# A rotation kernel: the last 2 MB loaded by two transfers, and slabs 2 and 3 stored in 1 MB halves

## Chip, cores, metric

One core of a Trainium2 chip. The metric is the device time of one execution in microseconds (us); below, "time" is the median of the runs of one kernel. A transfer is carried by 16 DMA engines in packets, and has landed when all 16 have reported; SyncE is the engine that issues the transfers, HBM the memory that holds the arrays, PSUM a second on-chip memory. The profile's own span is about 1.8 us shorter than the device time.

## The reference

```python
x = np.random.randn(32, 3, 256, 256).astype(np.float32)      # 25.17 MB
out = np.rot90(x, k=-1, axes=(-2, -1))                       # each 256 x 256 image turned by 90 degrees
```

Nothing is computed. Each byte is read once and written once: 50.33 MB in all, plus the rearranging between.

## The kernel before

The 96 images are handled as twelve slabs of 2 MB. Each slab has its own on-chip buffer, so all loads can be issued at once. VectorE transposes slab n into the buffer of slab n-1, whose contents it has already used; slab 0 goes to PSUM and is copied back at the very end, over the buffer of the last slab.

```python
    for n in range(n_slabs):                      # loads
        if n == last:
            nc.sync.dma_start(out=units[n], in_=ld8_v[n])            # 2 MB, two 8 KB rows per partition
            continue
        for i in range(I):                                           # I = 2: 1 MB each
            if n == 0:
                nc.sync.dma_start(out=units[n][:, i], in_=ld8_v[n][:, i])          # 128 x 8 KB
            else:
                nc.sync.dma_start(out=units[n][i::I]..., in_=ld16_v[n, i])         # 64 x 16 KB

    for n in range(n_slabs):
        ...                                       # two VectorE transposes: t_in -> t_out
        if n == 1:                                # stores
            nc.sync.dma_start(out=st_v[n][:, 0, :W], in_=t_out[:, 0, :W])          # 128 KB
            nc.sync.dma_start(out=st_v[n][:, 0, W:], in_=t_out[:, 0, W:])          # 896 KB
            nc.sync.dma_start(out=st_v[n][:, 1], in_=t_out[:, 1])                  # 1 MB
        elif n:
            nc.sync.dma_start(out=st_v[n], in_=t_out)                              # 2 MB

    for i in range(I):
        nc.scalar.copy(out=units[last][:, i], in_=turned0[:, i])
    nc.sync.dma_start(out=st_v[0], in_=units[last])
```

(Three dots mark cuts.) All transfers are issued by SyncE in this order. The built program gives them eight completion semaphores in turn, so each issue first waits until the transfer eight places earlier has landed.

Of the kernel before, what the change touches and what calls it, by code (L numbers as in the profile page):

```python
# [1 line left out]

# [4 lines left out]




@with_exitstack
def kernel(
    ctx: ExitStack,
    tc: tile.TileContext,
    x: bass.AP,
    out: bass.AP,
):

















    nc = tc.nc
    fp32 = mybir.dt.float32

    B, C, H, W = x.shape
    P = nc.NUM_PARTITIONS  # L40
    RI, RO = 16, 8
    K = H // RI
    I = 2
    Q = P // (K * I)
    n_slabs = B * C // (Q * I)
    last = n_slabs - 1
    F = RO * W

    rows_in = x.rearrange("b c h w -> (b c h) w")
    rows_out = out.rearrange("b c h w -> (b c h) w")  # L50
    ld8_v = rows_in.rearrange("(n i p r) w -> n p i (r w)", i=I, p=P, r=RO)
    ld16_v = rows_in.rearrange("(n i m r) w -> n i m (r w)", i=I, m=Q * K, r=RI)
    st_v = rows_out.rearrange("(n i p c) w -> n p i (c w)", i=I, p=P, c=RO)

    pools = [ctx.enter_context(tc.tile_pool(name=f"unit{u}", bufs=1)) for u in range(n_slabs)]
    units = [pool.tile([P, I, F], fp32, name=f"u{u}") for u, pool in enumerate(pools)]
    psum = ctx.enter_context(tc.tile_pool(name="psum", bufs=1, space=bass.MemoryType.PSUM))
    turned0 = psum.tile([P, I, F], fp32, name="turned0")

    for n in range(n_slabs):  # L60
        if n == last:
            nc.sync.dma_start(out=units[n], in_=ld8_v[n])
            continue
        for i in range(I):
            if n == 0:
                nc.sync.dma_start(out=units[n][:, i], in_=ld8_v[n][:, i])  # L66
            else:
                nc.sync.dma_start(out=units[n][i::I].rearrange("p i f -> p (i f)"), in_=ld16_v[n, i])

    for n in range(n_slabs):  # L70
        t_in, t_out = units[n], units[n - 1] if n else turned0
        if n in (0, last):
            for i in range(I):
                src = t_in[:, i].rearrange("p (r g c) -> p c r g", r=RO, c=RO)
                dst = t_out[:, i].rearrange("p (c g r) -> p c r g", c=RO, r=RO)
                nc.vector.transpose(out=dst[:, :, ::-1, ::-1], in_=src)  # L76
        else:
            src = t_in.rearrange("p i f -> p (i f)").rearrange("p (r g c) -> p c r g", r=RI, c=RO)
            dst = t_out.rearrange("p i (c k r) -> p c r k i", c=RO, r=RI)[:, :, ::-1, ::-1, :]
            for h in range(2):  # L80
                cs = slice(h * RO // 2, (h + 1) * RO // 2)
                nc.vector.transpose(out=dst[:, cs], in_=src[:, cs])  # L82

        if n == 1:
            nc.sync.dma_start(out=st_v[n][:, 0, :W], in_=t_out[:, 0, :W])
            nc.sync.dma_start(out=st_v[n][:, 0, W:], in_=t_out[:, 0, W:])
            nc.sync.dma_start(out=st_v[n][:, 1], in_=t_out[:, 1])
        elif n:
            nc.sync.dma_start(out=st_v[n], in_=t_out)  # L89

# [5 lines that stand above are left out]
# [1 line left out]
_INS = ['x']  # L97
_OUTS = [((32, 3, 256, 256), 'float32')]


# [23 lines left out]
```

## Time and profile before

| | before |
|---|---|
| time, us | 124.06 (3 runs, 123.96 to 124.23) |
| DMA engines busy | 97.8% |
| VectorE busy | 76% |
| transfers | 37 (23 loads, 14 stores) |
| last store issued, landed, us | 101.15, 121.18 |

Read the DMA share and the GB/s per slice first: they show whether the bytes flow without a break. Then read who issues the transfers and what each issue waits for. The lines for that are in the prediction. One view it names without showing it is the chain of waits, of the kernel before, by engine:

```profile
DMA 57%; DVE 13%; issue 7%; DVEq 3%; ACT 2%; SPq 1%
```

### The profile page before, as it was taken

The numbers are of one execution on the slowest core, as the hardware profiler recorded it, in microseconds if no ns is written. First come the engines' busy times: TensorE is split into PE (matmuls) and PEld (weight loads), VectorE is DVE, ScalarE is ACT, GpSimd is POOL, SyncE is SP. The second block draws the span as 40 slices with busy tenths as digits, with TensorE's granted clock in tenths as the row PEclk, the third lists the DMA queues.
The fourth block names the chain that finished last, engine by engine and source line by source line (L and its number), as shares of the span: only waits on it lengthen the run. The fifth ranks groups of instructions, "written<-read, shape, count | busy, mean of one in ns | idle before, by whom it ended". The sixth has DMA issues, their size and how long they took to land.

```text
span 122.2 us, 134 instructions
## 1 busy us (share of the span) xinstructions
DVE 93.3 (76%) x24; ACT 5.0 (4%) x3; POOL 0.2 (0%) x4
## 2 busy tenths in 40 slices
DVE  0299999999999999999999999999999940000000
ACT  0000000000000000000040000000000651000000
POOL 0000000000000000000000000000000000000000
DMA  3999999999999999999999999999999999999993
GB/s 88 429 432 434 440 440 429 429 429 429 429 429 429 429 429 424 434 424 408 370 414 428 426 429 429 429 429 429 429 429 429 424 429 429 429 429 426 429 429 166
DMA packets 5584, 50.33 MB, mean 412 GB/s; under 512 B 592, under 2 KB 720, under 8 KB 848
## 3 DMA queue, kind: packets, MB, share of 16 engines
q1 hardware_dynamic: 5584, 50.33, 97.8%
HBM read 25.17 MB, written 25.17 MB: 412 GB/s over the span
## 4 chain that ended last, share of the span: by engine, by line
DMA 57%; DVE 13%; issue 7%; DVEq 3%; ACT 2%; SPq 1%
DMA u<-in_x_dram 39%; DMA out_dram<-u 18%; DVE u L82 10%; DVE u L76 3%; DVEq L119 3%; ACT u L92 2%; SPq L66 1%; SPq L89 0%
## 5 line engine op out<-in xcount | busy, mean ns | idle before, releaser
L82 DVE STREAM_TRANSPOSE u<-u 128x2048 f32<-128x2048 f32 x20 | 78.0, 3948 | 0.3
L76 DVE STREAM_TRANSPOSE turned<-u 128x2048 f32<-128x2048 f32 x2 | 7.6, 3828 | 5.5 <-DMA u<-in_x_dram 5.5
L76 DVE STREAM_TRANSPOSE u<-u 128x2048 f32<-128x2048 f32 x2 | 7.8, 3953 | 0.0
L92 ACT COPY u<-turned 128x2048 f32<-128x2048 f32 x2 | 3.7, 1866 | 33.8 <-DVE u L76 33.8
L92 ACT ACT_TABLE_LOAD x1 | 1.3, 1283 | 62.4 <-DMA u<-in_x_dram 62.4
L108 POOL MEMSET const-bfloat16-1.0<- 128x1 bf16 x1 | 0.1, 102 | 0.0
L108 POOL MEMSET const-uint8-127<- 128x1 uint8 x1 | 0.1, 102 | 0.0
L108 POOL MEMSET const-float32-0.0<- 128x1 f32 x1 | 0.1, 99 | 0.2 <-issue 0.2
L108 POOL MEMSET const-float32-1.0<- 128x1 f32 x1 | 0.1, 99 | 0.0
## 6 DMA issues: line engine op xcount, KB each, us to landing
u<-in_x_dram SPq DMA_DIRECT2D x22, 1024.0 KB, 19.6
out_dram<-u SPq DMA_DIRECT2D x11, 2048.0 KB, 25.0
u<-in_x_dram SPq DMA_DIRECT2D x1, 2048.0 KB, 22.5
out_dram<-u SPq DMA_DIRECT2D x1, 1024.0 KB, 20.2
out_dram<-u SPq DMA_DIRECT2D x1, 896.0 KB, 20.2
out_dram<-u SPq DMA_DIRECT2D x1, 128.0 KB, 20.6
```

Of the source, the lines that this page charges most:

```text
L66: nc.sync.dma_start(out=units[n][:, i], in_=ld8_v[n][:, i])
L76: nc.vector.transpose(out=dst[:, :, ::-1, ::-1], in_=src)
L82: nc.vector.transpose(out=dst[:, cs], in_=src[:, cs])
L92: nc.scalar.copy(out=units[last][:, i], in_=turned0[:, i])
L108: nc = _bacc.Bacc("TRN2", target_bir_lowering=False, num_devices=1)
L119: with _tile.TileContext(nc) as tc:
```

## The change

In the kernel before, the 2 MB load is one entry in the rotation of eight, and so are the 2 MB stores behind it. The change cuts that load and the stores of slabs 2 and 3 into 1 MB halves, so that SyncE meets transfers of one size while the work turns from loading to storing, and half of the last slab is announced earlier.

```diff
@@ -58,11 +58,8 @@
     turned0 = psum.tile([P, I, F], fp32, name="turned0")
 
     for n in range(n_slabs):
-        if n == last:
-            nc.sync.dma_start(out=units[n], in_=ld8_v[n])
-            continue
         for i in range(I):
-            if n == 0:
+            if n in (0, last):
                 nc.sync.dma_start(out=units[n][:, i], in_=ld8_v[n][:, i])
             else:
                 nc.sync.dma_start(out=units[n][i::I].rearrange("p i f -> p (i f)"), in_=ld16_v[n, i])
@@ -85,6 +82,9 @@
             nc.sync.dma_start(out=st_v[n][:, 0, :W], in_=t_out[:, 0, :W])
             nc.sync.dma_start(out=st_v[n][:, 0, W:], in_=t_out[:, 0, W:])
             nc.sync.dma_start(out=st_v[n][:, 1], in_=t_out[:, 1])
+        elif n in (2, 3):
+            for i in range(I):
+                nc.sync.dma_start(out=st_v[n][:, i], in_=t_out[:, i])
         elif n:
             nc.sync.dma_start(out=st_v[n], in_=t_out)
```

## The prediction

> **What bounds the kernel now.** I began with the busy summary, the slices and the queue totals of the page, because a kernel that only rearranges data is either bound by its transfers or by the engine that rearranges.
>
> ```profile
> DVE 93.3 (76%) x24; ACT 5.0 (4%) x3; POOL 0.2 (0%) x4
> DMA  3999999999999999999999999999999999999993
> GB/s 88 429 432 434 440 440 429 429 429 429 429 429 429 429 429 424 434 424 408 370 414 428 426 429 429 429 429 429 429 429 429 424 429 429 429 429 426 429 429 166
> DMA packets 5584, 50.33 MB, mean 412 GB/s; under 512 B 592, under 2 KB 720, under 8 KB 848
> q1 hardware_dynamic: 5584, 50.33, 97.8%
> ```
>
> The 16 DMA engines are busy for 97.8% of the span and hold 429 GB/s in nearly every slice; VectorE is busy for 76%. 50.33 MB at 429 GB/s take 117.3 us of the 122.2 us span. The other 4.9 us are all that better scheduling of the same bytes could get, and the slices say where they lie. The first slice (3.05 us) moves at 88 instead of 429 GB/s and so loses 2.4 us; the last one, at 166, loses 1.9 us. In the middle there is one dip, slices 18 to 22 counted from one (424, 408, 370, 414, 428): 101 GB/s short in total, 101/429 of a slice, 0.7 us. Part of that is bookkeeping, since a packet is counted where it starts; finer windows give the real size:
>
> ```profile
> 20.00:54.00 34.00, 33.83 (x10) 0.00 (x0) 0.00 (x0) 1.00 1.01 432
> 59.00:61.50 2.50, 2.46 (x2) 0.00 (x0) 0.00 (x0) 1.00 0.96 342
> 64.00:101.00 37.00, 35.09 (x10) 3.61 (x2) 0.00 (x0) 1.00 1.01 428
> ```
>
> (Stretch, its length, VectorE, ScalarE, GpSimd, clock, DMA share, GB/s.) Loads alone run at 432, stores alone at 428, and the 2.5 us at the end of the last load run at 342: 2.5 x (1 - 342/428) = 0.50 us lost. The DMA share stays at 0.96 there, so the engines are not without work; their packets take longer. The packet records agree: an 8 KB packet takes 309 ns nearly everywhere, and 359 and 416 ns on average of those that start between 59 and 60 and between 60 and 61 us. The completion times say it too: 1 MB loads land 2.45 us apart, the last of them at 56.89, and the 2 MB load at 62.29, 5.40 us later instead of 4.90.
>
> Next I read the issue order, which is where the change acts. All transfers go through SyncE, in program order, on eight completion semaphores used in turn, so that transfer k is issued only when transfer k-8 has landed. Single windows of the timeline:
>
> ```profile
> 49.60 0.38 SPq L89 DMA_DIRECT2D out_dram<-u  x1
> 52.06 0.38 SPq L89 DMA_DIRECT2D out_dram<-u  x1
> 54.51 2.09 SPq L89 DMA_DIRECT2D out_dram<-u  x1
> 56.95 2.13 SPq L89 DMA_DIRECT2D out_dram<-u  x1
> 62.35 1.51 SPq L89 DMA_DIRECT2D out_dram<-u  x1
> 75.80 0.37 SPq L89 DMA_DIRECT2D out_dram<-u  x1
> 101.15 0.37 SPq L93 DMA_DIRECT2D out_dram<-u  x1
> ```
>
> The issue of a store takes 0.37 to 0.38 us, but those of slabs 4, 5 and 6 take 2.09, 2.13 and 1.51 us. These are the three issues with most still queued: counting packets issued and not yet finished, 1392 were in flight after the quick issue at 52.06, and 1510, 1654 and 1545 after the slow ones, whose end comes as earlier packets drain. I read this as a queue that is full at some 1400 to 1600 packets. It holds up SyncE; whether it also has to do with the slow packets at 59 to 61 us, the profile does not say.
>
> Last, the waits of SyncE and the end. The final store is issued at 101.15, after VectorE's last slab (99.2) and ScalarE's copy, and lands at 121.18: it stands 20 us in the queue behind stores issued earlier.
>
> ```profile
> SPq L119 <- DMA out_dram<-u: 19.7, 1, 19.7
> SPq L89 <- DVE u L82: 26.3, 5, 7.4
> ```
>
> So VectorE, ScalarE and SyncE all finish 20 us ahead, and the end is simply when the queue has carried its bytes. The chain of waits on the page, which puts 13% on VectorE and 7% on "issue", follows releases back and does not contradict this: that time lies under queued transfers.
>
> **What the Trainium skill says.** "DMA: Bandwidth & Descriptors", section Where 436 GB/s comes from, gives 435 GB/s as the ceiling of the 16 engines' ports. The trace agrees: 428 to 432 in steady state, 98 to 99% of it. Its section Rules for kernel authors asks for 128 partitions and at least 1 MiB per transfer; the new pieces are exactly 1 MB over 128 partitions, and the trace has such transfers already (both loads of slab 0, and the store of the second half of slab 1: landing 2.46 and 2.43 us after the one before, that is at full rate). "Perfetto Trace Analysis", section DMA Optimizations, says that splitting may help where DMA engines are generally idle; here they are not. The section Queues, rings and completion order of the first page describes completion as one semaphore write per engine, after that engine's data. The trace shows 592 packets under 512 B = 37 transfers x 16, each of 4 B and 9 ns.
>
> **The change part by part.** The order of instructions on VectorE is unchanged. SyncE issues 40 transfers instead of 37: the last load as 2 x 1 MB, slabs 2 and 3 as 2 x 1 MB each (the first stored slab was in pieces already). Bytes, 8 KB packets and addresses are the same; only the order of the two halves of a row pair within an engine's share may differ.
>
> Added on the queue: 3 transfers x 1 completion packet per engine x 9 ns = 0.03 us. This is on the path, and is all the direct cost.
>
> Added on SyncE: 3 issues x some 0.37 us = 1.1 us, beside the queue and with 20 us of slack at the end: 0.
>
> Moved: the stores. Three more entries in the rotation make every later store wait for a more recent transfer. Landings at 2.45 us per MB (slot 22 at 56.9; the halves of the last load at about 59.4 and 61.9) give: the first three stores at about 44.7, 47.1 and 49.6 (before 42.3, 44.7, 47.1), the halves of slabs 2 and 3 at 52.0, 54.5, 56.9 and 59.4, slab 4 at about 61.9 (before 54.5), slab 5 at about 62.6 (before 56.9), slab 6 at about 64.6 (before 62.35), slab 7 at 68.0, when VectorE has it. From there VectorE's 7.85 us per slab (2 x 3.9) sets the issue as before: 75.8, 83.6, 91.5, 99.2, and 101.15 for slab 0. Does the queue run dry? When the loads end, slabs 1 to 3 are issued: 6 MB, 14.7 us of work, up to about 76.5. By 68.0 slabs 4 to 7 are in, which reach to about 96; slab 8 is in at 75.8, and so on. It never comes within 10 us of empty. So the delay of slabs 4 to 6 costs nothing.
>
> Removed: the crowding. At about 59.4 us I count 24 to 31 outstanding, 8 x 144 = some 1150 packets less those done, and with slabs 4 and 5 issued about 1300 to 1400. The two long issues at 54.5 and 56.9 should go; a shorter one may come at about 64.6 for slab 6, where seven outstanding and the new one come to near 1500.
>
> Sum: +0.03 us, and between 0 and -0.5 us for the dip, according to whether the slow packets come from the crowded queue (or from the 2 MB load's order) or from the turn from loads to stores, which stays. I give the removal about one chance in three: 0.03 - 0.33 x 0.5 = -0.14 us, so 124.06 becomes about 123.9.
>
> **The rivals.**
> First, the dip goes entirely. For it: the slow packets begin at 59.3 us, just after the two slowest issues, and they belong to the one load that has two rows per partition. Against it: the first ten packets of each engine of that load run at 311 to 314 ns while the queue is as full, and the stores with the same two-row shape take 309 ns. It would make 123.5 to 123.6 us.
>
> Second, nothing changes in the queue: the slow packets are the last three to five loads of each engine, just where the engine's next work is stores, and the turn has to be made in either kernel. That makes 124.1 us. It is my main case.
>
> Third, a new wait: the rotation of eight now spans less data, so SyncE reaches each store later. A starved queue would need the 14.7 us of stores at hand at 62 us to run out before slab 4 comes at 62, which the waits make impossible; only a store issued over 10 us late would show, and VectorE is ahead until 68 us. I see no way to 2% (2.5 us) here. A smaller loss, 0.2 to 0.4 us, could come if VectorE's and the transfers' traffic met differently at the turn.
>
> Fourth, the earlier arrival of half of the last slab helps VectorE. It cannot: VectorE turns to that slab at 91.5 us, and the load has landed at 62.3.
>
> **Range and chances.** A gain of over 2% would have to bring the time below 121.6 us; even with the dip gone the queue carries 117.3 us of bytes and the ramps at both ends stay. A loss of over 2% needs 2.5 us without work for the DMA engines. Three runs of before spread over 0.27 us. So 123.9 us, 123.4 (dip gone and a favourable run) to 124.4 (no gain and a small loss at the turn); within 2% nearly certainly.
>
> **What would show it.** Steps right: 640 packets under 512 B instead of 592; a queue share of about 98%; the last store issued at about 101.2 and landing some 20 us later; issues of slabs 4 and 5 at about 62 us; slices of 429 GB/s outside the middle. The long issues of SyncE gone or later. The slices around 59 to 61 us decide between the first two rivals: near 429 there means the crowding (or the order in the load) made the dip, near 370 means the turn. The prediction is wrong if a slice after the middle falls well below 429 (starvation), or if 8 KB packets of the split transfers take other than 309 ns.

## The result, and the profile after

| | before | after |
|---|---|---|
| time, us (6 runs each, in the same rounds) | 124.09 (123.96 to 124.23) | 123.97 (123.77 to 124.08) |
| ratio after / before | | 0.9988, 95% interval 0.9975 to 1.0001 |
| transfers | 37 | 40 |
| packets under 512 B | 592 | 640 |
| last store issued, landed, us | 101.15, 121.18 | 101.27, 121.46 |

A ratio is the mean time of one kernel's fast runs over that of the other's of the same rounds, so it is not quite the ratio of the medians quoted beside it. The page of the changed kernel:

```profile
DVE 93.3 (76%) x24; ACT 5.0 (4%) x3; POOL 0.2 (0%) x4
DMA  3999999999999999999999999999999999999994
GB/s 118 418 450 429 429 429 429 429 429 429 429 429 429 429 429 429 429 429 391 359 413 429 429 429 426 429 421 429 429 429 429 429 429 429 429 429 426 429 429 180
DMA packets 5632, 50.33 MB, mean 412 GB/s; under 512 B 640, under 2 KB 768, under 8 KB 896
q1 hardware_dynamic: 5632, 50.33, 97.8%
DVE 47%; issue 27%; DMA 4%; DVEq 3%; ACT 2%
```

The dip is where it was (391, 359, 413), and the rest is at 429 as before. The last line is the chain of waits again: it now puts 47% on VectorE and 4% on transfers, although nothing about the end has changed. The chain follows whatever released the last issue, and the issues of SyncE are released now by a landing, now by VectorE; here it happened to stay on VectorE all the way back. A chain that runs underneath a full queue is not a bound.

The three stretches that the prediction read, now of the kernel after (stretch, length, VectorE, ScalarE, GpSimd, clock, DMA share, GB/s):

```profile
20.00:54.00 34.00, 33.83 (x10) 0.00 (x0) 0.00 (x0) 1.00 1.00 424
59.00:61.50 2.50, 2.47 (x2) 1.28 (x1) 0.00 (x0) 1.00 1.01 330
64.00:101.00 37.00, 35.21 (x10) 3.48 (x2) 0.00 (x0) 1.00 1.01 428
```

330 against 342 GB/s: the slow stretch at the end of the loads is still there. The completion times agree: the second half of the last load lands 2.99 us after the first half, where other 1 MB loads take 2.45. So 0.54 us is lost there, against 0.50 before. (The 424 in the first row is a matter of where packets start: up to 49.8 us the loads still land 2.44 to 2.54 us apart.)

The issue of the stores of slabs 4, 5, 6, 7, 8 and 0, from single windows of the timeline of the kernel after:

```profile
62.67 0.39 SPq L89 DMA_DIRECT2D out_dram<-u  x1
63.27 0.54 SPq L89 DMA_DIRECT2D out_dram<-u  x1
65.21 0.77 SPq L89 DMA_DIRECT2D out_dram<-u  x1
68.08 2.31 SPq L89 DMA_DIRECT2D out_dram<-u  x1
75.91 0.37 SPq L89 DMA_DIRECT2D out_dram<-u  x1
101.27 0.37 SPq L93 DMA_DIRECT2D out_dram<-u  x1
```

Slab 4 is issued 8.2 us later than before (62.67 instead of 54.51) and slab 5 6.3 us later, at no cost, since the queue is full of earlier stores. The two issues of over 2 us at 54.5 and 56.95 are gone. One of 2.31 us has appeared at 68.08, again at no cost.

### The profile page after: what moved, and what is told of

Same layout as the page of the kernel before. It is cut to its first block, busy times and chain, and to the rows that moved or that the text cites. A ratio compares the mean times of both kernels' runs of the same rounds, so it can differ in the third digit from the quotient of the medians.

```text
span 122.3 us, 138 instructions
## 1 busy us (share of the span) xinstructions
DVE 93.3 (76%) x24; ACT 5.0 (4%) x3; POOL 0.2 (0%) x4
## 3 DMA queue, kind: packets, MB, share of 16 engines
q1 hardware_dynamic: 5632, 50.33, 97.8%
## 4 chain that ended last, share of the span: by engine, by line
DVE 47%; issue 27%; DMA 4%; DVEq 3%; ACT 2%
DVE u L79 37%; DVE turned L73 6%; DMA u<-in_x_dram 4%; DVE u L73 3%; DVEq L119 3%; ACT u L92 2%
```

## The experiments

Twelve runs followed: ten new kernels, and the kernel after and one of the new ones once more; all gave the right result. A number used throughout is the **excess of the last load**: how much later it lands than the load before it, less 2.45 us for 1 MB or 4.90 us for 2 MB. A load has landed when the slowest of the 16 engines has finished its share, so the excess follows the slowest engine. "In flight" counts the packets issued and not yet finished.

### 1. Only the load split (load_only)

```diff
# against the kernel after
-        elif n in (2, 3):
-            for i in range(I):
-                nc.sync.dma_start(out=st_v[n][:, i], in_=t_out[:, i])
```

> Only the last load is split; all stores of slabs 2 to 11 stay at 2 MB. Turn theory (the slow load packets come from the change from loads to stores and cost 0.5 us in any kernel): the last 1 MB load lands 2.9 to 3.0 us after the one before it, time 124.0 to 124.1. Row-order theory (alternating between the two halves of the 2 MB load slows its packets): the last two loads land 2.45 us apart each, time 123.5 to 123.6. Crowding theory: the queue is still crowded, so the dip stays too; long issues of SyncE of over 1.5 us remain.

123.89 us against 123.87 for before in the same rounds, ratio 0.9999 (0.9981 to 1.0017). The last load lands 2.81 us after the one before: excess 0.36 us. So it is not the alternation between two rows of a partition that slows the packets. One expectation missed: only one long issue was left, of 1.17 us at 62.43. The issue of slab 5 at 59.61 took 0.37 us although 1621 packets were in flight after it. In the kernel before, an issue that ended at 1510 took 2.09 us. So "the queue is full at 1400 to 1600 packets" is not the rule behind the long issues.

### 2. Only the stores split (store_only)

```diff
# against the kernel before
+        elif n in (2, 3):
+            for i in range(I):
+                nc.sync.dma_start(out=st_v[n][:, i], in_=t_out[:, i])
         elif n:
```

> Only slabs 2 and 3 are stored in halves; the last load stays one 2 MB transfer. Turn theory: the 2 MB load lands about 5.4 us after the load before, time 124.0 to 124.1. Crowding theory: as the queue holds less by then, the dip shrinks below 0.3 us, time below 123.9.

123.80 us, ratio 0.9991 (0.9974 to 1.0008). The 2 MB load lands 5.30 us after the load before, excess 0.40 us, although at most 1237 packets were in flight until it had landed, instead of 1654. The slow packets stay without the crowd. The time is where the crowding theory had it (below 123.9 us), but so is that of the kernel before in these rounds (123.87 us), so it decides nothing.

### 3. Every store in halves (all_halves)

```diff
# against the kernel after; slab 0's store is split likewise
-        elif n in (2, 3):
+        elif n > 1:
             for i in range(I):
                 nc.sync.dma_start(out=st_v[n][:, i], in_=t_out[:, i])
-        elif n:
-            nc.sync.dma_start(out=st_v[n], in_=t_out)
```

> The change taken further: every store in 1 MB halves, 48 transfers with the last load split. At most 8 x 144 = 1152 packets in flight, so no issue of SyncE over 0.8 us. Turn theory: the dip of 0.5 us stays; 8 more completion packets per engine than the changed kernel cost 0.07 us; time 124.0 to 124.2. Crowding theory: the dip goes, 123.5 to 123.6. A rival against my claim that queue depth does not matter: with only 8 MB in flight the queue runs thin and the time rises by over 0.5 us.

123.96 us, ratio 1.0001 (0.9984 to 1.0017). The excess of the last load is 0.52 us. (It has 49 transfers, not 48: 784 packets under 512 B.) At most 8 MB were in flight throughout, and the time is the same: the depth of the queue does not matter down to there. Missed: issues of over 0.8 us did occur, with only some 1050 packets in flight. Windows of its timeline, at two places:

```profile
62.41 0.33 SPq L87 DMA_DIRECT2D out_dram<-u  x1
62.80 0.95 SPq L87 DMA_DIRECT2D out_dram<-u  x1
...
91.93 1.25 SPq L87 DMA_DIRECT2D out_dram<-u  x1
```

Each long issue here begins less than 0.1 us after the end of another, while those that come alone take 0.33 us. That fits the early issues too: the back-to-back loads of 1.6 to 5.4 us took 0.5 to 0.6 us, the later ones 0.47. It does not explain the 2.31 us at 68.08 in the kernel after, nor the 2.09 us at 54.51 in the kernel before, which came alone. What makes an issue long stays open; that it costs nothing here is shown by every kernel above.

### 4. Two turns from loads to stores (two_turns)

```diff
# against the kernel before: the last load moves behind the stores of slab 1
-            nc.sync.dma_start(out=units[n], in_=ld8_v[n])
             continue
...
             nc.sync.dma_start(out=st_v[n][:, 1], in_=t_out[:, 1])
+            nc.sync.dma_start(out=units[last], in_=ld8_v[last])
```

> The 2 MB load of the last slab is issued behind the stores of slab 1, so that the queue turns from loads to stores twice (and once back). Same bytes, same number of transfers (37). Turn theory, cost per turn from loads to stores 0.5 us: two dips instead of one, time 124.5 to 124.6, more if the turn back costs as well. If the cost is paid once, or belongs to crowding: 124.0 to 124.1 and one dip.

124.46 us against 123.87, ratio 1.0044 (1.0026 to 1.0061): 0.5 to 0.6 us more for one more turn. Stretches of its profile:

```profile
54.00:57.00 3.00, 3.00 (x2) 0.00 (x0) 0.00 (x0) 1.00 0.92 322
57.00:64.00 7.00, 6.96 (x2) 0.00 (x0) 0.00 (x0) 1.00 1.02 426
64.00:67.00 3.00, 3.00 (x2) 0.00 (x0) 0.00 (x0) 1.00 0.98 358
67.00:101.00 34.00, 32.17 (x9) 4.81 (x3) 0.00 (x0) 1.00 1.01 428
```

There are two dips, each ahead of a turn to stores, and between them, where the queue turns back from stores to loads, 426 GB/s. The first dip belongs to an ordinary 64 x 16 KB load, which landed 3.07 us after the one before it, so the last slab's load has nothing special. Packet by packet, with what each load packet took beyond its usual time, the engines lose 0.46 us on average at the first dip and 0.44 us at the second, and between them every store packet takes its usual time. This is the run that settles what the dip belongs to.

### 5. No small pieces behind the loads (no_small)

```diff
# against the kernel before
-            nc.sync.dma_start(out=st_v[n][:, 0, :W], in_=t_out[:, 0, :W])
-            nc.sync.dma_start(out=st_v[n][:, 0, W:], in_=t_out[:, 0, W:])
+            nc.sync.dma_start(out=st_v[n][:, 0], in_=t_out[:, 0])
```

> The kernel before with the first half of slab 1 stored as one transfer of 1 MB instead of 128 KB and 896 KB, so that no 1 KB packets stand right behind the loads. Turn theory: the 2 MB load still lands about 5.4 us after the one before it, time 124.0 to 124.1. Small-packet theory (the engines run ahead into 1 KB packets and slow the loads): it lands 4.9 us after, time 123.5 to 123.6.

124.11 us against 123.88, ratio 1.0016 (0.9994 to 1.0039). The load lands 5.52 us after the one before, excess 0.62 us. The 1 KB packets are not the cause.

### 6. An on-chip copy between the loads and the stores (copy_turn)

```diff
# against the kernel before; pad is a new tile of 128 x 4 KB
         if n == 1:
+            nc.sync.dma_start(out=pad, in_=t_out[:, 0, : F // 2])
```

> The kernel before with an added transfer of 0.5 MB from one on-chip buffer to another (unused, the output stays right) queued between the last load and the first store. It should add its own 0.5 MB at 428 GB/s, 1.2 us: 125.2 to 125.4. If the slow load packets come from the engines' turning to on-chip reads, the load before the copy is slow by 0.5 us as before; if they come from the writes to the HBM, the load before the copy runs at 309 ns per packet and the copy or the first store is slow instead.

125.30 us against 123.88, ratio 1.0110 (1.0092 to 1.0128): 1.4 us for 0.5 MB, close to the 1.2 us of its bytes. The load in front of the copy lands 5.41 us after the one before it, excess 0.51 us. The copy lands 1.29 us later and the first store after it as usual. Stretches of its profile, around the load's end, the copy and the first stores:

```profile
57.00:59.00 2.00, 2.00 (x1) 0.00 (x0) 0.00 (x0) 1.00 1.03 430
59.00:61.50 2.50, 2.46 (x2) 0.00 (x0) 0.00 (x0) 1.00 0.93 336
61.50:62.80 1.30, 1.30 (x1) 0.32 (x1) 0.00 (x0) 1.00 0.99 404
62.80:64.00 1.20, 1.20 (x1) 0.96 (x1) 0.00 (x0) 1.00 1.11 445
```

The slow packets come just before the engines start to read on-chip memory. No write to the HBM is near: the first store is queued behind the copy. By this run the turn that costs is that of the source, from HBM to on-chip memory. How on-chip reads slow loads that come before them, no run shows.

### 7. Every store in eight pieces of 32 neighbouring partitions (pieces_256k)

```diff
# against load_only; the stores of slabs 1 to 11, and of slab 0 likewise
+            for j in range(4):
+                for i in range(I):
+                    ps = slice(32 * j, 32 * j + 32)
+                    nc.sync.dma_start(out=st_v[n][ps, i], in_=t_out[ps, i])
```

> The splitting exaggerated: every store in eight pieces of 32 partitions x 8 KB, 256 KB each, 96 stores instead of 15. The packets stay 8 KB. My cost per transfer is one completion packet of 9 ns on each engine: 81 more make 0.7 us, so 124.8, no long issues, SyncE busy 96 x 0.35 = 34 us. Rival (depth matters): with 8 x 256 KB = 2 MB in flight the completion delay[...] and the issue time show as gaps, and the time rises by over 2 us.

170.03 us, ratio 1.372. The first theory was far off. The rival's "over 2 us" came true, but not by the gaps it named: the store packets were still 8 KB, but after 70 us two in five of them took 600 to 650 ns and only three in ten the usual 309 (median 598), with the engines busy for 0.94 of the time. Missed too: SyncE's issues took 1.09 us in the median and up to 2.39. The Trainium skill, "SBUF — State Buffer", section Door 1: The DMA port swizzle, has a reason at hand: partitions 0 to 31, and 32 to 63 as well, reach only 8 of the 16 ports, for an asymptote of 218 GB/s. I had used 32 neighbours without looking there. One more thing is to be seen in this run: the last load has an excess of only 0.03 us. The engines turn to on-chip sources here too, but get their data from there at half the rate. That fits the idea that they read ahead into the stores' data and thereby slow the last loads; no run here tests it further.

### 8. The same pieces with every fourth partition (pieces_strided)

```diff
# against pieces_256k
-                    ps = slice(32 * j, 32 * j + 32)
+                    ps = slice(j, P, 4)
```

> The eight 256 KB pieces of the run pieces_256k (170 us, store packets of some 620 instead of 309 ns), but each piece takes every fourth partition instead of 32 neighbours. Depth, packet size, number of transfers and issue time are the same. If the 32 neighbouring partitions made the packets slow, they now take 309 ns and the time is 124.1 plus 81 completion packets of 9 ns, 124.8. If the thin queue (2 MB in flight) or the number of transfers made it slow, it stays near 170.

125.57 us against 124.08, ratio 1.0117 (1.0100 to 1.0134). The same stretch (69 to 100 us, stores alone), first of pieces_256k:

```profile
69.00:100.00 31.00, 30.27 (x8) 2.46 (x2) 0.00 (x0) 1.00 0.94 235
```

then of pieces_strided:

```profile
69.00:100.00 31.00, 30.23 (x8) 2.50 (x2) 0.00 (x0) 1.00 1.00 413
```

So the neighbouring partitions made the packets slow, and the trace agrees with the skill: 235 GB/s against its 218, which the run may pass because pieces of both halves of the partitions overlap where one follows the other (an estimate, not tested). The 1.5 us that remain are twice the 0.7 us that I had put down to 81 completion packets of 9 ns (counting the loads it is 120 transfers instead of 37, 83 more). What sets the pace here is SyncE. Its waits, and its issues of the pieces of slabs 1 to 11, in pieces_strided:

```profile
SPq L85 <- DMA u<-in_x_dram: 16.0, 8, 2.3
L85 SPq DMA_DIRECT2D out_dram<-u x88: 468/595/883, 44.9 to 115.3; - x88
```

Only the first eight pieces wait, each for a load; no later piece waits for an earlier one to land. From 78 us on SyncE issues one piece every 0.64 us, 0.60 of it in the issue itself (as long as the first loads issued back to back), and 256 KB in 0.64 us are 410 GB/s, where the trace has 413. The engines alone would need 2 x 309 + 9 = 627 ns per piece, close behind. The queue is thin (some 140 packets in flight, later 128) because SyncE does not fill it faster. The store packets took 309 ns in the median until 76 us and 313 to 315 from 80 us on, 0.8 us more per engine in all; whether that is slower memory or waiting for SyncE, the trace does not say. So the run prices SyncE's issues, not the completion packets. With 8 MB in flight (run 3) neither showed.

### 9. The second load issued from ScalarE (act_start)

```diff
# against the kernel after
-                nc.sync.dma_start(out=units[n][:, i], in_=ld8_v[n][:, i])
+                (nc.scalar if (n, i) == (0, 1) else nc.sync).dma_start(out=units[n][:, i], in_=ld8_v[n][:, i])
```

> The changed kernel with the second load (slab 0, half 1) issued from ScalarE at the same time as the first from SyncE. It tests where the 2.4 us of the first slice go: half of the engines start their first packet only at 2.4 us, 0.65 us after the others. If issue time is the limit, all start by about 1.8 us and the time falls by 0.2 to 0.4 us to 123.6 to 123.8; if not, 124.0.

123.54 us against 123.88, ratio 0.9971 (0.9956 to 0.9986). The ratio is to the kernel before, so what the change itself gains, if anything, is in it. The time is what I had hoped for (0.06 us below the range), the reason is not. The start got no faster: the third load lands at 10.76 us, in the kernel after at 10.52. And VectorE starts its first transpose at 8.5 instead of 5.6 us, because the two loads of slab 0 now share the engines and land together. The last load lands 2.48 us after the one before, excess 0.03 instead of 0.54 us, so by this measure the saving is at the turn.

### 10. The same with nothing of the change (act_before)

```diff
# against the kernel before
-                nc.sync.dma_start(out=units[n][:, i], in_=ld8_v[n][:, i])
+                (nc.scalar if i else nc.sync).dma_start(out=units[n][:, i], in_=ld8_v[n][:, i])
```

> The kernel before, with nothing of the change, and the second load issued from ScalarE. In act_start the gain of 0.3 us did not come from the start (load 3 landed 0.2 us later than in the changed kernel) but from the turn to stores, where the last load took 2.48 instead of 2.99 us. If the second queue at the start is what spares the turn, this kernel also reaches 123.5 to 123.6 and its 2 MB load lands 4.9 to 5.0 us after the one before; if it was the change together with it, it stays at 123.9.

123.80 us against 124.08, ratio 0.9971 (0.9958 to 0.9983). The same ratio as in run 9, so the gain does not need the change. The 123.5 to 123.6 us expected were missed, in rounds on another chip where the kernel before took 124.08 instead of 123.88. The 2 MB load lands 5.02 us after the one before, excess 0.12 us. Slices of the page of act_before:

```profile
GB/s 97 403 457 430 430 430 430 430 430 430 430 430 430 430 430 424 419 430 403 408 411 427 430 430 430 427 430 430 430 430 427 427 430 424 430 430 430 430 427 177
```

The dip is down to 403, 408, 411, from 408, 370, 414.

### 11 and 12. The kernels after and act_start once more (after_again, act_again)

No edit: the same sources, in the same rounds as runs 8 and 10.

> The changed kernel once more, in the same rounds as the others, for a second profile of the turn and a second ratio. If the size of the dip belongs to the kernel: the last load again lands 2.9 to 3.0 us after the one before, and the excess of packet time between 59 and 62 us is again 0.5 to 0.6 us on average. If it varies from run to run as the engines' lags do: anything from 0.15 to 0.6 us. Ratio 0.998 to 1.000.

123.82 us against 124.08, ratio 0.9973 (0.9957 to 0.9989). The excess of the last load is 0.44 us. The excess of packet time between 59 and 62 us is 0.36 us on average over the engines, where the first profile of this kernel had 0.59: the mean size of the dip varies from run to run.

> The run act_start once more. If its gain is real: 123.4 to 123.7, ratio 0.996 to 0.998, the last load again 2.5 us after the one before it. If it was the luck of one chip or one profile: 123.8 to 124.0.

123.46 us, ratio 0.9951 (0.9937 to 0.9965). The last load's excess is 0.24 us, not the 0.05 expected. The 2.5 us stretch at the turn, of act_again:

```profile
59.00:61.50 2.50, 2.50 (x1) 1.28 (x1) 0.00 (x0) 1.00 0.97 382
```

It was 388 in act_start and 392 in act_before. In the eight profiles of kernels 1, 2, 3, 5, 6, before and after (twice) it was 330 to 375; only the kernels with 32-partition stores were higher (pieces_strided 387, pieces_256k 426). The gain of the second queue is small: 0.3% in act_before, and 0.2% in act_again when it is set against after_again of the same rounds (means 123.53 and 123.81 us), since its 0.9951 holds what the change gained there too. In those rounds the change alone (0.9973) gained as much as the second queue alone (0.9971). Kernels with the second queue were faster than the kernel before in three of three runs, with intervals clear of 1, and act_start is the fastest of all.

Why does the turn cost less then? One thing that the traces show is the lag between the first and the last of the 16 engines to finish a transfer. In the kernel before it is 0.25 us all through the loads and 0.60 to 0.71 us for every store after the turn. In act_before it is 0.64 to 0.67 us during the loads and 0.50 us at the last store. The end is set by the last engine. So one could think that an engine that already lags loses less at the turn. But this is only an order of events, and the kernel after contradicts it: its loads lag by 0.63 to 0.86 us, and its excess is 0.54 us (load_only: 0.56 and 0.36). Lag does not decide it.

Nor is the saving plainly at the turn once the average of the 16 engines is taken instead of the slowest. On average the last load of act_before lands when that of the kernel before does (61.99 and 61.98 us), its third load having landed 0.19 us later (10.44 against 10.25); in act_again it lands 0.19 us earlier than in after_again (61.87 and 62.06). And all_halves, with one queue, lost 0.15 us of packet time on average between 59 and 62 us, as little as the three runs with two queues (0.13 to 0.15), while its slowest engine lost 0.52. The cause stays open.

## Why the prediction was right

The prediction was 123.9 us (123.4 to 124.4), "within 2% nearly certainly". 123.97 us came out, ratio 0.9988.

- **The bound.** Right. 97.8% queue share in both kernels. A check that the prediction did not have: runs 9, 10 and 12 start VectorE 2.5 to 2.9 us later, and the time does not rise. VectorE's slack is real.
- **Direct cost.** The 640 packets under 512 B came as worked out. The 0.03 us cannot be seen in the times. Pieces_strided, meant to enlarge this cost, does not measure it, since SyncE's issues set the pace there (run 8). It stays an estimate.
- **Moved stores.** Right in kind: slabs 4, 5, 6 and 7 were predicted at 61.9, 62.6, 64.6 and 68.0 and were issued at 62.67, 63.27, 65.21 and 68.08. Slabs 4 to 6 came 0.6 to 0.8 us late mostly because I had not put the turn's own 0.5 us into the landing of the last load (62.61 instead of 61.9). The queue did not run dry.
- **Crowding.** Half wrong. The long issues at 54.5 and 56.9 went, but the one left over came at slab 7 (2.31 us at 68.08), not at slab 6 (0.77 us). The rule behind it, a queue full at 1400 to 1600 packets, fell in runs 1 and 3. The kernel before already spoke against it: its issue of slab 7, at 67.96, took only 0.50 us and left 1541 packets in flight, as many as the 1.51 us issue of slab 6, so slabs 4 to 6 were not alone in having the most queued.
- **The dip.** The main case, rival two, held: the turn stays, 0.50 us before and 0.54 and 0.44 us after. Rival one fell: neither the row order (run 1), nor the crowd (runs 2 and 3, and the kernel after itself, with at most 1111 packets in flight by then), nor the small packets (run 5) makes it. The prediction put the slow packets at the very end of the load; in its trace they start between 59 and 61 us, and the load packets after that take 309 to 313 ns again. Run 4 has two turns, two dips and 0.5 to 0.6 us more. The term of -0.14 us in the sum was one third of the dip's removal, which did not happen in either profile; that the medians differ by 0.12 us, and that 123.97 lies so near 123.9, is luck and no confirmation of it.
- **Is there a gain at all?** Open. The two comparisons gave 0.9988 (up to 1.0001) and 0.9973 (up to 0.9989), and the change's halves alone 0.9999 and 0.9991, both with 1 inside. A gain of 0.1 to 0.3% is possible. No view of the profile shows where it would lie.

## What to carry to other kernels

When the transfers are busy for 98% of the time, as here, and the last store stands 20 us in the queue, cutting the same bytes into other transfers moves waits about and leaves the time. What is left to win is at the edges of the flow, here a fast start, the turn from loads to stores (0.5 us each, so turn once), and the end. When you do cut a transfer, cut so that each piece still reaches partitions all over the memory: 32 neighbours per piece cost 37%, every fourth partition 1.2%. And leave the issuing engine room: at one 256 KB piece per 0.64 us it was SyncE that set the pace.

## What the Trainium skill lacked or had wrong

- "DMA: Bandwidth & Descriptors": it has nothing on the turn from loads to stores. One queue loses 0.5 us of its slowest engine's time just before it goes from HBM sources to on-chip ones (excess 0.50 us before, 0.54 after; 0.5 to 0.6 us more of total time with a second turn), and nothing in the packets' times when it goes back (426 GB/s).
- "DMA: Bandwidth & Descriptors", section Rules for kernel authors: it advises against spreading transfers over several issuing engines for bandwidth, as this only saves issue time. Issuing one early load from ScalarE took 0.2 to 0.3% off (act_before 0.9971 to the kernel before; act_again 123.53 us to 123.81 of after_again), and not by an earlier start: the third load landed no earlier. The cause is open.
- No page that I looked up says when an issue by SyncE takes 2 us instead of 0.37 us; here issues of over 2 us ended with 1454 to 1654 packets in flight, in pieces_256k one of 2.39 us with 184, and one of 0.37 us with 1621.
- "SBUF — State Buffer", section Door 1: The DMA port swizzle, gives an asymptote of 218 GB/s for 32 neighbouring partitions; here back-to-back stores of that shape ran at 235, and at 413 from 32 spread ones, a case for which it has no measurement.
